# Gated outputs stored whole and split where they are read back, and weight factors made 512 columns at a time, in a gated pooling and recurrence block

## The chip, the cores and the metric

The kernel runs on one core of a Trainium2 chip. The metric is the device time of one execution in microseconds (us). The engines that matter here are TensorE (PE, which multiplies matrices and loads their weights), VectorE (DVE) and ScalarE (ACT), which work element by element, and SyncE (SP), on which this kernel issues nearly all its transfers. They run side by side, each in the order of its own list of instructions, and wait for each other through semaphores.

## The reference

One layer over 2048 tokens of 1024 channels: a norm, one wide projection h @ w_in, a pooling branch (branch A), a gated linear recurrence with 8 heads of 128 channels (branch B), a merge of both by sigmoid gates, an output projection and a residual. All is float32.

```python
def reference(x, c, w_ada, b_ada, g_pre, g_post, w_in, pool_w, pool_scale, lb_logits,
              hgrn_norm_g, w_pool_o, w_hgrn_o, w_out):
    ...
        h = rms_norm(x, g_pre[l]) * (1.0 + scale) + shift
        (pv, pg, hq, hf, hi, hg, mg_pool, mg_hgrn) = jnp.split(h @ w_in[l], split_idx, axis=-1)

        pooled = multiscale_pool(pv)
        pooled = jnp.einsum('bsgc,gcd->bsgd', pooled, pool_w[l].astype(jnp.float32))
        pooled = pooled.reshape(b, s, POOL_WIDTH) * pool_scale[l]
        branch_a = (pooled.astype(x.dtype) * jax.nn.silu(pg)) @ w_pool_o[l]
        ...
        f = lb + (1.0 - lb) * jax.nn.sigmoid(zf)
        ...
        o = hgrn2(q, k, v, logf)
        o = rms_norm(o, hgrn_norm_g[l]).astype(x.dtype).reshape(b, s, HGRN_WIDTH)
        branch_b = (o * jax.nn.silu(hg)) @ w_hgrn_o[l]

        merged = jax.nn.sigmoid(mg_pool) * branch_a + jax.nn.sigmoid(mg_hgrn) * branch_b
        y = merged @ w_out[l]
        x = x + gate * rms_norm(y, g_post[l])
```

The outputs that are gated, and that this change is about, are `pooled * silu(pg)` (called P in the kernel, 4 groups of 128 channels) and `o * silu(hg)` (called G, 8 heads of 128 channels).

## The kernel before

**Products.** Every large product is made from numbers split in two: `hi` is the value rounded to TensorE's fp32r form, `lo` what is missing. `split` makes the first on ACT with a copy and the second on DVE with a subtraction:

```python
    def split(src32, hi, lo, e=None):
        return A.copy(hi, src32), (e or V).tensor_tensor(lo, src32, hi.bitcast(F32), op=SUB)
```

`three` then multiplies hi by hi, hi by lo and lo by hi, so that one 128 by 512 by 128 product costs three matmuls. On top of it, blocks of two by two are multiplied with seven products in place of eight (a scheme of Strassen's kind). That is `quad` for the columns of w_in, and `rows7` for the projections to V and y of pass 1. The seven weight factors of such a block are sums and differences of its four quarters, named "11", "21", "12", "22" and "s1".

**Stages.** There are two passes (`p`) of 1024 tokens, each of two halves (`t`) of T = 512. In each pass V is made first. Then come the eight heads: for each head three quads, `fq` (gate f and q), `m` (the two merge gates, whose sigmoids go to DRAM as `Sd`) and `gp` (gate of the head, and pooling value or pooling gate). The last head has `gp` ahead of `m`. Between the products of a quad, `htick` runs a step of the recurrences of the head (`hgrn`, a generator for each half), so that the recurrence of head h runs inside the quads of head h and of the head behind. At its end it makes G (tile `sgg`, line 813). After the heads stand the **a jobs** (`a_job`, j = 0 to 7: P times w_pool_o, two halves of twelve matmuls each into the banks psA, then `sm` = psA times the sigmoid), the **b jobs** (the same with G and w_hgrn_o), and the projection to y.

**Gated outputs.** `two_out` splits an output. The last head's G and the last group's P stay on the chip. The others (heads 0 to 6, groups 0 to 2) are stored to the DRAM tiles Gd and Pd as hi and lo, two stores for each half. `two_in` reads them back: P in steps of the last head's `m` quad (`tick_in` takes one at each of the ticks, after two empty ones), G of head j - 1 ahead of the a job j.

**Weights.** `take` hands out the next weight and prepares four ahead (LOOK). In pass 0 a weight is loaded raw into `wr` (a pool of seven), combined on DVE where it is a factor, split into `whl` (a pool of four), and stored to DRAM as `scr_...`. Pass 1 reads these back, hi and lo in one load of 512 KB. For the projections to V and y in pass 1, the factors "v7" and "y7" are made beforehand by `row_factors`, whose 56 small steps hang behind the heads: "v7" in pass 0 and "y7" in pass 1. `htick` takes one at two of every five ticks:

```python
            if every[0] % 5 in (1, 3):
                once(behind_heads)
```

One group of seven steps is a load of two tiles (`ra`, `rb`), an empty step, and five steps of a sum and one or two splits (`put`). It works on 256 columns, hi and lo side by side in one tile `rf`. There are eight groups.

**What sets the order.** Each engine runs its instructions in program order as a scheduler laid them out, which puts an instruction where it expects its inputs to be ready. SP issues all transfers in one order. A transfer that waits for its data or for a free buffer holds those behind it. `gated` loads are placed behind the last store. All small tiles come from one pool of 76 (`utile`), the banks of the quads and of psA from a pool of four. In the profile L175 is the subtraction of `split` (or its copy on ACT), L109 a store, L179 a raw weight load, L461 (`tt`) any product, sum or difference of two tiles, L331 a matmul, L251 the sum that makes "s1" of a weight quad, and L684 and L690 the masked copies of the recurrence's scores.

## Time and profile before

| | us |
|---|---|
| median of three runs | 1799.85 |
| the three runs | 1799.85, 1803.84, 1798.95 |
| profiled execution, its own time | 1797.54 |
| span of its profile | 1795.8 |
| mean granted TensorE clock | 0.999 |
| heads of pass 0 | about 100 to 690 |
| a jobs of pass 0 | about 690 to 752 |
| heads of pass 1 | about 1016 to 1566 |
| a jobs of pass 1 | about 1566 to 1626 |

The profile is of one execution. Its page gives the busy time of each engine over the span. The trace behind it answers what one stretch of time, one tile or one wait holds. A row of a wait names the instruction that waited, its line, and what it waited for ("PE pagp L331 <- DVE c22gp L461"), then the total in us, the count and the longest. A row of the timeline gives the start in us, the time from start to end (neighbours may overlap), the engine (SPq is the queue of SP), the line, the operation, output and inputs, and the shape; a wait ahead of it stands in brackets.

### The profile page before, as it was taken

To read this page: it belongs to the slowest core of one execution; us is meant where nothing else is said; L and a number is where in the kernel's file an instruction comes from. 1 tells how busy PE (TensorE), PEld (TensorE's weight loads), DVE (VectorE), ACT (ScalarE), POOL (GpSimd) and SP (SyncE) were. 2 spreads that over 40 slices of the span, in tenths; PEclk is the share of its full clock that TensorE was granted. 3 is DMA by queue.
4 is the path that set the end of the run, shared out by engine and by line. 5 is a ranking of instruction groups with operands and counts; after the bars stand their busy time and mean duration, and the time that the engine had idled before them with its cause. 6 is when DMAs were issued, how large, how long until landed. Compare 5 with 4: busy or idle time off the path is not lost.

```text
span 1795.8 us, 32263 instructions
## 1 busy us (share of the span) xinstructions
PE 1753.0 (98%) x11997; PEld 1434.1 (80%) x11997; DVE 1161.1 (65%) x2522; ACT 801.1 (45%) x1925; POOL 80.6 (4%) x144
## 2 busy tenths in 40 slices
PE   7999999999999999999999999999999999999998
PEld 4787887888787787888878788888888888888886
DVE  3758898897888895475536166666666665633446
ACT  5746657566565563222433144354454453310041
POOL 1100000000000010000000000000000000000002
PEclk9999999999999999999999999999999999999999
DMA  9768787888878769997987886876877866696367
GB/s 316 255 198 292 272 295 288 277 304 281 285 271 300 265 213 318 336 323 257 320 294 249 281 254 199 282 249 215 274 228 238 280 206 238 201 351 209 129 204 258
DMA packets 270902, 471.49 MB, mean 263 GB/s; under 512 B 21101, under 2 KB 144666, under 8 KB 270746
## 3 DMA queue, kind: packets, MB, share of 16 engines
q1 hardware_dynamic: 270746, 469.44, 77.1%
q8 instruction: 94, 1.54, 0.4%
q14 instruction: 62, 0.51, 0.1%
HBM read 275.90 MB, written 193.46 MB: 261 GB/s over the span
## 4 chain that ended last, share of the span: by engine, by line
PE 62%; DMA 5%; DVE 2%; ACT 1%; issue 1%; SPq 0%; POOL 0%; DVEq 0%; ACTq 0%
PE psB L331 10%; PE pagp L331 6%; PE pam L331 6%; PE pafq L331 5%; PE psA L331 4%; PE psy L331 4%; PE pegp L331 3%; PE pefq L331 3%; PE pem L331 3%; PE psa L331 2%; PE ray L331 2%; PE po L331 2%; PE raV L331 2%; PE pbm L331 2%; PE pbfq L331 1%; PE pbgp L331 1%
## 5 line engine op out<-in xcount | busy, mean ns | idle before, releaser
L175 ACT CAST whl<-wr 128x512 fp32r<-128x512 f32 x192 | 118.5, 621 | 131.0 <-PE psB L331 24.7
L175 DVE TENSOR_TENSOR whl<-wr,whl 128x512 fp32r<-128x512 f32 x192 | 130.9, 688 | 64.2 <-ACT whl L175 55.2
L331 PE MATMUL psB<-Gh,whl 128*128 128x512 f32 x512 | 158.6, 390 | 0.0
L331 PE MATMUL pagp<-hT,whl 128*128 128x512 f32 x384 | 128.5, 395 | 4.7 <-DVE c22gp L461 3.8
L331 PE MATMUL pam<-hT,whl 128*128 128x512 f32 x384 | 129.5, 398 | 1.2 <-DVE c22m L461 1.2
L331 PE MATMUL pafq<-hT,whl 128*128 128x512 f32 x384 | 126.7, 391 | 3.3 <-ACT c12fq L592 3.3
L331 PEld LDWEIGHTS psB<-Gh,whl 128*128 128x128 f32 x512 | 96.1, 188 | 20.5 <-issue 0.5
L690 DVE COPY_PREDICATED PT<-mask,psa 128x256 f32<-128x256 uint8 x160 | 86.4, 550 | 36.1 <-PE psa L331 36.0
L331 PE MATMUL psB<-Gl,whl 128*128 128x512 f32 x256 | 100.0, 391 | 0.0
L331 PEld LDWEIGHTS pagp<-hT,whl 128*128 128x128 f32 x384 | 72.0, 188 | 21.9 <-issue 3.1
L331 PEld LDWEIGHTS pafq<-hT,whl 128*128 128x128 f32 x384 | 72.1, 188 | 19.5 <-ACT c12fq L592 4.4
L331 PEld LDWEIGHTS pam<-hT,whl 128*128 128x128 f32 x384 | 72.1, 188 | 17.2 <-DVE c22m L461 1.6
L331 PE MATMUL psA<-Ph,whl 128*128 128x512 f32 x256 | 82.5, 397 | 3.1 <-DMA Ph<-Pd 1.9
L331 PE MATMUL psV<-whl,hB 128*128 128x512 f32 x256 | 79.9, 394 | 2.4 <-ACT hB L175 2.4
L461 DVE TENSOR_TENSOR K<-K,TT 128x256 f32<-128x256 f32 x192 | 81.0, 426 | 1.8 <-PE psa L331 1.7
L331 PE MATMUL psy<-whl,mgh 128*128 128x512 f32 x256 | 80.4, 394 | 0.5 <-DVE y L461 0.5
L331 PE MATMUL pam<-lT,whl 128*128 128x512 f32 x192 | 74.9, 390 | 0.0
L331 PE MATMUL pagp<-lT,whl 128*128 128x512 f32 x192 | 74.9, 390 | 0.0
L331 PE MATMUL pafq<-lT,whl 128*128 128x512 f32 x192 | 74.7, 389 | 0.0
L331 PEld LDWEIGHTS psa<-X,K 128*32 128x32 f32 x2816 | 49.6, 110 | 25.8 <-issue 24.4
L461 DVE TENSOR_TENSOR sm<-psB,sm 128x512 f32<-128x512 f32 x32 | 22.0, 689 | 64.4 <-PE psB L331 63.9
L331 PE MATMUL psa<-X,K 128*32 128x48 f32 (+2 forms) x2816 | 60.3, 208 | 0.2 <-DVE PT L684 0.2
(471 smaller groups left out, 4417.2 us busy)
## 6 DMA issues: line engine op xcount, KB each, us to landing
wr<-in_w_in_dram SPq DMA_DIRECT2D x112, 256.0 KB, 5.0
whl<-scr_y SPq DMA_DIRECT2D x40, 512.0 KB, 4.9
sm<-Sd SPq DMA_DIRECT2D x64, 256.0 KB, 4.8
scr_v<-rfv SPq DMA_DIRECT2D x56, 256.0 KB, 2.8
whl<-scr_v SPq DMA_DIRECT2D x28, 512.0 KB, 3.7
scr_y<-rfy SPq DMA_DIRECT2D x56, 256.0 KB, 3.3
x<-in_x_dram SPq DMA_DIRECT2D x32, 256.0 KB, 4.9
wa<-in_w_ada_dram SPq DMA_DIRECT2D x32, 256.0 KB, 6.0
```

Source lines behind the costliest of these rows:

```text
L175: return A.copy(hi, src32), (e or V).tensor_tensor(lo, src32, hi.bitcast(F32), op=SUB)
L331: return PE.matmul(o, lhsT=l, rhs=r, start=start, stop=stop, skip_group_check=True)
L461: return (e or V).tensor_tensor(o, a, b, op=op)
L690: V.copy_predicated(dst.rearrange("p (c q) a b -> p c q a b", c=NT), m, src.rearrange("p c (a b) -> p c a b", b=b).unsqueeze(2) .broadcast ...
```

## The change

It has two parts. **Gated outputs**: `two_out` stores the output as it is (one store of 256 KB for each half in place of two, and the DRAM tiles are half as large). `two_in` reads it into the tile that will be `lo`, and the new `two_split` makes hi from it on ACT and then lo in place on DVE. For P the three splits are steps of the last head's `m` quad behind the loads (one empty step fewer, and what is left over is run after the quad); for G the split of head j - 2 is called ahead of the a job j, and that of head 6 after the last a job. What stays on the chip is split as before. **Weight factors**: `row_factors` works on 512 columns, in four groups of fourteen steps, with four loads of 256 KB, one operation of 512 columns in place of two of 256, and hi and lo in two tiles with a store each. The number of steps stays 56.

```diff
@@ -256,47 +256,41 @@
     def row_factors(key, src, e):
 
         steps = []
-        W = T // 2
         for i in range(4):
-            for c0 in (0, W):
-                r = {}
-
-                def put(f, nm, i=i, c0=c0, r=r):
-                    w = utile(f"rf{key}{f}{i}{c0}", F32R)
-                    hi, lo = w[:, 0:W], w[:, W:T]
-                    split(r[nm], hi, lo, e)
-                    if (key, f, i) not in scr:
-                        scr[key, f, i] = dram(f"scr_{key}_{f}_{i}", [P, 2 * T])
-                    store((key, f, i), scr[key, f, i].rearrange("p (z n) -> p z n", z=2)[:, :, c0:c0 + W],
-                          w.bitcast(F32).rearrange("p (z n) -> p z n", z=2))
-
-                def ld(i=i, c0=c0, r=r):
-                    a, b = utile(f"ra{key}{i}{c0}"), utile(f"rb{key}{i}{c0}")
-                    for w, k in ((a, 2 * i), (b, 2 * i + 1)):
-                        SP.dma_start(w.rearrange("p (z n) -> p z n", z=2),
-                                     src[k * P:(k + 1) * P, :].rearrange("p (z n) -> p z n", z=2)[:, :, c0:c0 + W])
-                    r.update({"11": a[:, 0:W], "21": a[:, W:T], "12": b[:, 0:W], "22": b[:, W:T]})
-
...
-                steps += [ld, nop, lambda two=two: two((0, "11"), (1, "12")),
-                          lambda two=two, a=sums: two(a, (2, "s1")),
-                          lambda two=two, a=sums2: two(a, (3, "11")),
-                          lambda two=two, a=sums3: two((4, "21"), a),
-                          lambda two=two: two((5, "12"), (6, "22"))]
+            r = {}
+
+            def ld(i=i, r=r):
+                for nm, k, z in (("11", 0, 0), ("21", 0, 1), ("12", 1, 0), ("22", 1, 1)):
+                    r[nm] = utile(f"ra{key}{i}{nm}")
+                    SP.dma_start(r[nm], src[(2 * i + k) * P:(2 * i + k + 1) * P, z * T:(z + 1) * T])
+
+            def put(f, nm, i=i, r=r):
+                w = [utile(f"rf{key}{f}{i}{z}", F32R) for z in range(2)]
+                split(r[nm], w[0], w[1], e)
+                scr[key, f, i] = dram(f"scr_{key}_{f}_{i}", [P, 2 * T])
+                for z in range(2):
+                    store((key, f, i), scr[key, f, i][:, z * T:(z + 1) * T], w[z].bitcast(F32))
+
+            def sums(r=r, i=i):
+                r["s1"] = utile(f"rs{key}{i}")
+                tt(r["s1"], r["21"], r["22"], op=ADD, e=e)
+
+            def sub(o, a, b, r=r):
+                tt(r[o], r[a], r[b], op=SUB, e=e)
+
+            nop = lambda: None
+            steps += [ld, nop, nop,
+                      lambda put=put: put(0, "11"),
+                      sums,
+                      lambda put=put: put(1, "12"),
+                      lambda put=put: put(2, "s1"),
+                      lambda sub=sub: sub("21", "11", "21"),
+                      lambda sub=sub: sub("11", "s1", "11"),
+                      lambda put=put: put(3, "11"),
+                      lambda put=put: put(4, "21"),
+                      lambda sub=sub: sub("12", "12", "11"),
+                      lambda put=put: put(5, "12"),
+                      lambda put=put: put(6, "22")]
         return steps
 
     early = {}
@@ -952,19 +946,24 @@
 
     def two_out(nm, p, i, t, src, cx, stay):
 
-        hi, lo = utile(f"{nm}h{p}_{i}_{t}", F32R), utile(f"{nm}l{p}_{i}_{t}", F32R)
-        split(src, hi, lo)
         if stay:
+            hi, lo = utile(f"{nm}h{p}_{i}_{t}", F32R), utile(f"{nm}l{p}_{i}_{t}", F32R)
+            split(src, hi, lo)
             cx["g" + nm][i, t] = (hi, lo)
         else:
-            for z, w in enumerate((hi, lo)):
-                store((nm, i), cx[nm + "d"][i][:, t, z, :], w.bitcast(F32))
+            store((nm, i), cx[nm + "d"][i][:, t, :], src)
 
     def two_in(nm, p, i, cx):
         for t in range(2):
-            cx["g" + nm][i, t] = tuple(utile(f"{nm}{z}{p}_{i}_{t}", F32R) for z in "hl")
-            for z, w in enumerate(cx["g" + nm][i, t]):
-                gated(w.bitcast(F32), cx[nm + "d"][i][:, t, z, :], (nm, i))
+            hi, lo = utile(f"{nm}h{p}_{i}_{t}", F32R), utile(f"{nm}l{p}_{i}_{t}", F32R)
+            raw = lo.bitcast(F32)
+            gated(raw, cx[nm + "d"][i][:, t, :], (nm, i))
+            cx["g" + nm][i, t] = (hi, lo)
+
+    def two_split(nm, i, cx):
+        for t in range(2):
+            hi, lo = cx["g" + nm][i, t]
+            split(lo.bitcast(F32), hi, lo)
 
     def sig_in(p, j, w, cx):
 
@@ -1155,9 +1154,9 @@
                               "mv", "y", "yss")}
         cx["Vd"] = dram(f"Vd{p}", [P, 8, D])
         for h in range(NH):
-            cx["Gd"][h] = dram(f"Gd{p}_{h}", [P, 2, 2, T])
+            cx["Gd"][h] = dram(f"Gd{p}_{h}", [P, 2, T])
         for g in range(NG):
-            cx["Pd"][g] = dram(f"Pd{p}_{g}", [P, 2, 2, T])
+            cx["Pd"][g] = dram(f"Pd{p}_{g}", [P, 2, T])
         for j in range(KT):
             for w in range(2):
                 cx["Sd"][j, w] = dram(f"Sd{p}_{j}_{w}", [P, 2, T])
@@ -1378,10 +1377,13 @@
                     quad("gp" + n, cx, gp, htick)
                 else:
                     if h == NH - 1:
-                        steps += [lambda: None] * 2
+                        steps += [lambda: None]
                         steps += [lambda g=g: two_in("P", p, g, cx) for g in range(NG - 1)]
+                        steps += [lambda g=g: two_split("P", g, cx) for g in range(NG - 1)]
                     quad("m" + n, cx, lambda row, t, u: m_got(p, h, row, t, u, cx), tick_in)
                 htick()
+            while steps:
+                once(steps)
             if p + 1 < NPASS:
                 x_stats(8 + h)
         while behind_heads:
@@ -1390,7 +1392,10 @@
         for j in range(KT):
             if j > 0:
                 two_in("G", p, j - 1, cx)
+            if j > 1:
+                two_split("G", j - 2, cx)
             a_job(p, j, cx)
+        two_split("G", NH - 2, cx)
         while active:
             tick()
         sums = []
```

The lines above 300 of the changed kernel stand six lines earlier: the masked copies at 684 and 690 are at 678 and 684, `tt` is at 455, the line of G at 807.

The scheduler lays the whole program out anew. Three places are shown. The first is DVE in head 4 of pass 0, in the `gp` quad, where G of head 3 is finished (sgg0_3). `whl133` and `whl134` are weight factors of this quad, `wrpv2_1` is one of its raw tiles, Gh and Gl are hi and lo of G, and rfv is a factor for V. Before:

```order
L813 SCALAR_TENSOR_TENSOR sgg0_3_0_4649<-pot0_3_0_5281,vec_102,sgg0_3_0_4649 128x512
L813 SCALAR_TENSOR_TENSOR sgg0_3_1_4591<-pot0_3_1_5293,vec_102,sgg0_3_1_4591 128x512
L175 TENSOR_TENSOR whl133_5312<-wrpv2_1_4960,whl133_5312 128x512
L175 TENSOR_TENSOR Gl0_3_0_5288<-sgg0_3_0_4649,Gh0_3_0_5287 128x512
L251 TENSOR_TENSOR wrpv2_1_4960<-wrpv2_1_4960,wrpv2_0_4953 128x512
L175 TENSOR_TENSOR Gl0_3_1_5300<-sgg0_3_1_4591,Gh0_3_1_5299 128x512
L175 TENSOR_TENSOR rfv732256_5306<-rav72256_4887,rfv732256_5306 128x256
L175 TENSOR_TENSOR whl134_5332<-wr13021_5196,whl134_5332 128x512
L690 COPY_PREDICATED PT0_141<-mask_98,psa0_0_1334 128x128x2
```

After:

```order
L807 SCALAR_TENSOR_TENSOR sgg0_3_0_4550<-pot0_3_0_5177,vec_102,sgg0_3_0_4550 128x512
L807 SCALAR_TENSOR_TENSOR sgg0_3_1_4501<-pot0_3_1_5184,vec_102,sgg0_3_1_4501 128x512
L175 TENSOR_TENSOR whl133_5194<-wrpv2_1_4856,whl133_5194 128x512
L251 TENSOR_TENSOR wrpv2_1_4856<-wrpv2_1_4856,wrpv2_0_4849 128x512
L175 TENSOR_TENSOR whl134_5214<-wr13021_5092,whl134_5214 128x512
L684 COPY_PREDICATED PT0_141<-mask_98,psa0_0_1334 128x128x2
```

The two Gl splits and the piece of a V factor are gone from in front of the split of whl134. The same place on SP, where wr13722 and wr13712 are raw weights of the head's next quad, before:

```order
L109 DMA Sd0_4_1_172<-sgm0_4_1_5278 128x512
L109 DMA Gd0_3_154<-Gh0_3_0_5287 128x512
L109 DMA Gd0_3_154<-Gl0_3_0_5288 128x512
L109 DMA Gd0_3_154<-Gh0_3_1_5299 128x512
L109 DMA Gd0_3_154<-Gl0_3_1_5300 128x512
L109 DMA scr_v7_3_2_4598<-rfv732256_5306 256x1x256
L109 DMA scr_('gp', 4)_3_5315<-whl133_5312 128x1024
L109 DMA scr_('gp', 4)_4_5335<-whl134_5332 128x1024
L179 DMA wr13722_5464<-in_w_in_dram 128x4x128
L179 DMA wr13712_5466<-in_w_in_dram 128x4x128
```

After:

```order
L109 DMA Sd0_4_1_172<-sgm0_4_1_5174 128x512
L109 DMA Gd0_3_154<-sgg0_3_0_4550 128x512
L109 DMA Gd0_3_154<-sgg0_3_1_4501 128x512
L109 DMA scr_('gp', 4)_3_5197<-whl133_5194 128x1024
L109 DMA scr_('gp', 4)_4_5217<-whl134_5214 128x1024
L179 DMA wr13722_5348<-in_w_in_dram 128x4x128
L179 DMA wr13712_5350<-in_w_in_dram 128x4x128
```

Ahead of the two raw loads there stand two stores of G in place of four, and no store of a V factor. The second place is SP in head 6 of pass 0, in the `fq` quad. Its factors are stored as scr_('fq', 6), and wr165 names the four raw tiles of the `m` quad behind it. Before:

```order
L109 DMA scr_('fq', 6)_3_6497<-whl161_6494 128x1024
L109 DMA scr_('fq', 6)_4_6517<-whl162_6514 128x1024
L109 DMA scr_('fq', 6)_5_6536<-whl163_6533 128x1024
L109 DMA scr_v7_0_3_5830<-rfv703256_6552 256x1x256
L109 DMA scr_v7_1_3_5835<-rfv713256_6556 256x1x256
L109 DMA scr_('fq', 6)_6_6563<-whl164_6560 128x1024
L179 DMA wr16511_6579<-in_w_in_dram 128x4x128
L179 DMA wr16521_6581<-in_w_in_dram 128x4x128
L179 DMA wr16522_6583<-in_w_in_dram 128x4x128
L179 DMA wr16512_6585<-in_w_in_dram 128x4x128
```

After:

```order
L179 DMA wr16511_6426<-in_w_in_dram 128x4x128
L179 DMA wr16521_6428<-in_w_in_dram 128x4x128
L109 DMA scr_('fq', 6)_3_6345<-whl161_6342 128x1024
L109 DMA scr_('fq', 6)_4_6365<-whl162_6362 128x1024
L109 DMA scr_('fq', 6)_5_6384<-whl163_6381 128x1024
L179 DMA wr16522_6430<-in_w_in_dram 128x4x128
L109 DMA scr_v7_3_3_6404<-rfv7330_6400 128x512
L109 DMA scr_v7_3_3_6404<-rfv7331_6401 128x512
L109 DMA scr_('fq', 6)_6_6410<-whl164_6407 128x1024
L179 DMA wr16512_6432<-in_w_in_dram 128x4x128
```

Two of the four raw loads moved ahead of the stores of factors 3 to 5, a third ahead of the stores of the V factor and of factor 6; the fourth stays behind them. The third place is DVE at the start of the a jobs of pass 0, where the recurrence of head 7 fills PT from its scores and scales K. Before:

```order
L690 COPY_PREDICATED PT0_141<-mask_98,psa0_0_1334 128x32x8
L461 TENSOR_TENSOR K0_7_0_7582<-K0_7_0_7582,TT0_7_0_7653 128x32x8
L684 COPY_PREDICATED PT0_141<-mask_98,psa0_0_1334 128x16x16
L461 TENSOR_TENSOR K0_7_0_7582<-K0_7_0_7582,TT0_7_0_7653 128x16x16
L684 COPY_PREDICATED PT0_141<-mask_98,psa0_0_1334 128x16x16
L690 COPY_PREDICATED PT1_142<-mask_98,psa0_1_1335 128x32x8
L461 TENSOR_TENSOR K0_7_1_7589<-K0_7_1_7589,TT0_7_1_7661 128x32x8
L684 COPY_PREDICATED PT1_142<-mask_98,psa0_1_1335 128x16x16
L461 TENSOR_TENSOR K0_7_1_7589<-K0_7_1_7589,TT0_7_1_7661 128x16x16
L684 COPY_PREDICATED PT1_142<-mask_98,psa0_1_1335 128x16x16
L175 TENSOR_TENSOR whl203_8209<-wr203_8207,whl203_8209 128x512
```

After:

```order
L684 COPY_PREDICATED PT0_141<-mask_98,psa0_0_1334 128x32x8
L455 TENSOR_TENSOR K0_7_0_7416<-K0_7_0_7416,TT0_7_0_7487 128x32x8
L175 TENSOR_TENSOR Pl0_0_0_7861<-Pl0_0_0_7861,Ph0_0_0_7860 128x512
L175 TENSOR_TENSOR Pl0_0_1_7864<-Pl0_0_1_7864,Ph0_0_1_7863 128x512
L678 COPY_PREDICATED PT0_141<-mask_98,psa0_0_1334 128x16x16
L455 TENSOR_TENSOR K0_7_0_7416<-K0_7_0_7416,TT0_7_0_7487 128x16x16
L678 COPY_PREDICATED PT0_141<-mask_98,psa0_0_1334 128x16x16
L684 COPY_PREDICATED PT1_142<-mask_98,psa0_1_1335 128x32x8
L455 TENSOR_TENSOR K0_7_1_7423<-K0_7_1_7423,TT0_7_1_7495 128x32x8
L678 COPY_PREDICATED PT1_142<-mask_98,psa0_1_1335 128x16x16
L455 TENSOR_TENSOR K0_7_1_7423<-K0_7_1_7423,TT0_7_1_7495 128x16x16
L678 COPY_PREDICATED PT1_142<-mask_98,psa0_1_1335 128x16x16
L175 TENSOR_TENSOR Pl0_1_0_7887<-Pl0_1_0_7887,Ph0_1_0_7886 128x512
L175 TENSOR_TENSOR Pl0_1_1_7890<-Pl0_1_1_7890,Ph0_1_1_7889 128x512
```

The splits of P of groups 0 and 1 (Pl0_0, Pl0_1, halves 0 and 1) now stand among these operations, the first pair behind two of them and the second behind eight more. In pass 1 one more order matters: before, the split of a factor for y (rfy753256) stood on DVE ahead of c22m of head 6, and in the changed order the factor's split there (rfy7631) stands behind it.

12 lines of the change are left out of this document (removed).

## The prediction

> **What bounds the kernel now.** I read the page first, then busy time by stage, then who waited for whom, then the timeline around the longest waits. The page:
>
> ```profile
> span 1795.8 us, 32263 instructions
> PE 1753.0 (98%) x11997; PEld 1434.1 (80%) x11997; DVE 1161.1 (65%) x2522; ACT 801.1 (45%) x1925; POOL 80.6 (4%) x144
> ```
>
> TensorE (PE) is busy for 1753.0 of 1795.8 us, and the change takes no matmul away. All that can be gained or lost is idle time of PE, 42.8 us in the whole run. The stages that the change touches are the heads (100 to 690 us in pass 0, 1016 to 1566 in pass 1) and the a jobs behind them:
>
> ```profile
> 100.00:690.00 590.00, 579.47 (x4539) 476.84 (x4538) 502.27 (x1127) 358.47 (x869) 30.28 (x42) 1.00 0.80 275
> 690.00:752.00 62.00, 58.93 (x402) 47.94 (x401) 25.75 (x51) 16.73 (x50) 3.27 (x6) 1.00 0.99 346
> 1016.00:1566.00 550.00, 547.40 (x4376) 451.91 (x4376) 335.26 (x831) 246.36 (x643) 17.61 (x28) 1.00 0.73 240
> 1566.00:1626.00 60.00, 58.78 (x404) 48.11 (x403) 22.01 (x45) 10.72 (x38) 2.40 (x4) 1.00 0.96 348
> ```
>
> Behind each stretch stand its length and the busy time of PE, weight load, VectorE (DVE), ScalarE (ACT) and POOL, then the granted clock (1.00 throughout), the share of the DMA engines and GB/s. In the heads of pass 0 DVE is busy 502 of 590 us and nearly bounds them too; in the a jobs the DMA engines are full (0.99 and 0.96). PE's idle time there is 10.5, 3.1, 2.6 and 1.2 us. The waits of PE, in the same order of stages (us in total, times, longest):
>
> ```profile
> PE pagp L331 <- DVE c22gp L461: 3.8, 3, 1.9
> PE pafq L331 <- ACT c12fq L592: 3.3, 4, 1.4
> PE pvm L331 <- ACT KS L777: 2.3, 2, 1.5
> ...
> PE psA L331 <- DVE sm L461: 1.2, 2, 0.9
> PE pk L775 <- DVE K L461: 1.1, 2, 0.7
> PE psA L331 <- DMA Ph<-Pd: 0.8, 1, 0.8
> ...
> PE pbfq L331 <- DMA whl<-scr_('fq', 0)_3_1356: 1.4, 1, 1.4
> PE pam L331 <- DVE c22m L461: 1.2, 1, 1.2
> ...
> PE psA L331 <- DMA Ph<-Pd: 1.1, 1, 1.1
> PE psA L331 <- DMA Pl<-Pd: 0.2, 1, 0.2
> ```
>
> They sum to 9.4, 3.1, 2.6 and 1.3 us: 16.4 us is the pool.
>
> **The change part by part.** *Factors 512 columns at a time.* Fewer, longer pieces on DVE:
>
> ```profile
> 599.34 0.75 DVE L175 TENSOR_TENSOR rfv<-rbv,rfv 128x256 fp32r<-128x256 f32 x2
> 600.01 0.42 DVE L461 TENSOR_TENSOR sq<-X,TT 128x256 f32<-128x256 f32 x1
> ...
> 458.94 0.69 DVE L175 TENSOR_TENSOR Gl<-sgg,Gh 128x512 fp32r<-128x512 f32 x1
> 459.54 0.68 DVE L251 TENSOR_TENSOR wrpv<-wrpv,wrpv 128x512 f32<-128x512 f32 x1
> 460.14 0.69 DVE L175 TENSOR_TENSOR Gl<-sgg,Gh 128x512 fp32r<-128x512 f32 x1
> ```
>
> Durations overlap, so I count from start to start: two of 256 columns take 600.01 - 599.34 = 0.67, or 0.335 each; one of 512 takes 0.60. Each pass has 56 half splits and 32 half sums, now 28 and 16 whole ones: 88 x 0.335 = 29.5 becomes 44 x 0.60 = 26.4, 3.1 us less. DMA counts and bytes stay.
>
> *Gated outputs unsplit.* Each pass moves 20 splits (7 heads and 3 groups, two halves) out of the heads: 20 x 0.60 = 12 us of DVE. With the factors DVE falls from 502 to about 487 us in pass 0. SyncE (SP) issues 20 stores of 256 KB fewer there and 20 loads fewer in the a jobs: 5.2 of the 62 x 346 = 21.5 MB that moved in pass 0's, about a quarter. The 20 splits go to the a jobs, where DVE was busy 25.75 of 62 us and is to be 37.8.
>
> Busy time of DVE is not PE's, so the gain must come wait by wait. The longest wait of the heads, in head 4 of pass 0, starts with a weight load that is issued late:
>
> ```profile
> 461.08 0.69 DVE L175 TENSOR_TENSOR whl<-wr,whl 128x512 fp32r<-128x512 f32 x1
> 462.55 1.05 SPq L109 DMA_DIRECT2D scr_('gp', 4)_4_5335<-whl  x1
> 463.65 1.82 SPq L179 DMA_DIRECT2D wr<-in_w_in_dram  x2
> 468.76 0.69 DVE L241 TENSOR_TENSOR wr137s<-wr,wr 128x512 f32<-128x512 f32 x1 [2.01 <-DMA wr<-in_w_in_dram]
> 473.14 0.68 DVE L461 TENSOR_TENSOR c22gp<-pagp,c22gp 128x512 f32<-128x512 f32 x1
> 473.98 0.47 PE L331 MATMUL pagp<-hT,whl 128*128 128x512 f32 x1 [1.90 <-DVE c22gp L461]
> ...
> 614.92 0.69 DVE L241 TENSOR_TENSOR wr179s<-wr,wr 128x512 f32<-128x512 f32 x1 [2.48 <-DMA wr<-in_w_in_dram]
> ```
>
> Both Gl splits stand ahead of the split of whl134 (461.08), whose store stands ahead of the load on SP. The load lands late, DVE idles 2.01 us at wr137s, c22gp is queued behind it, and PE waits 1.90 us. In the changed order the two Gl splits (1.2 us) and two of the four Gd stores are gone ahead of that point, so the load leaves at least 1.2 us earlier. I take 1.5 of the 1.9 us; in head 6, the same place (wr179s, 2.48 us), 1.2 us.
>
> In head 6 the four loads of wr165 leave at 563.14, behind four stores and their splits:
>
> ```profile
> 561.62 1.46 SPq L109 DMA_DIRECT2D scr_('fq', 6)_6_6563<-whl  x1
> 563.14 2.69 SPq L179 DMA_DIRECT2D wr<-in_w_in_dram  x4
> 568.72 0.69 DVE L175 TENSOR_TENSOR whl<-wr,whl 128x512 fp32r<-128x512 f32 x1 [1.39 <-DMA wr<-in_w_in_dram]
> 573.13 1.05 PE L331 MATMUL pvm<-pwt,pvt 128*128 128x128 f32 x7 [1.53 <-ACT KS L777]
> ```
>
> Two of them now stand ahead of all four stores and a third ahead of the last. The whole 1.5 us should go. The third c22gp wait (3.8 - 1.9 - 1.5, from the other two) is DVE's load alone: 0.3. Heads of pass 0: -1.5 - 1.2 - 1.5 - 0.3 = **-4.5 us**.
>
> Pass 1's c22m wait is a factor split that waits for ScalarE in front of it:
>
> ```profile
> 1473.85 0.42 DVE L175 TENSOR_TENSOR rfy<-rby,rfy 128x256 fp32r<-128x256 f32 x1 [2.37 <-ACT rfy L175]
> 1474.20 0.68 DVE L461 TENSOR_TENSOR c22m<-pam,c22m 128x512 f32<-128x512 f32 x1
> ```
>
> In the changed order this factor's split stands behind c22m: **-1.2 us**.
>
> *The a jobs.* Three groups must now be split before the matmuls, a new wait on PE's path. The Pl0 subtractions stand on DVE behind a mask copy and a K product, those of group 1 behind eight more such operations.
>
> ```profile
> 693.62 0.43 DVE L690 COPY_PREDICATED PT<-mask,psa 128x256 f32<-128x256 uint8 x1 [1.83 <-PE psa L331]
> 693.83 0.50 PE L331 MATMUL psA<-Ph,whl 128*128 128x512 f32 x1
> 711.63 16.65 PE psA L331 x72
> ```
>
> The last row, of the chain of waits, gives 16.65 / 72 = 0.231 us a matmul. First split: 693.62 + 2 x 0.335 + 0.69 = 694.98, while PE has three matmuls from 693.83 and is done at 694.52, so 0.5 us of waiting. Group 1: two splits from 694.29, eight operations and 0.69: 694.29 + 1.20 + 2.68 + 0.69 = 698.86, against 694.98 + 12 x 0.231 = 697.75 and about half a microsecond of scores: 0.6. So +1.1 us, if P lands by 694; its loads are half as many and the same store now stands behind the first pair. Of the old 3.1 us the Ph and K waits (1.9) go, since the scores' operands are ready by then, and the sm wait stays. Pass 0: 1.1 - 1.9 = **-0.8**. In pass 1 DVE has no weights to split and group 0 is split before its scores, so group 1 costs about 0.3 instead of 1.3: **-1.0**. The 14 G splits cost nothing so long as they fit beside DVE's idle 24 us; with that cover gone they cost as in the slower rival.
>
> *What is late next.* Some 2500 DVE rows change their order. Below, the 5 us of pass 0 that I left alone (9.4 - 4.5) could shrink as well; above, each of ten waits on DVE or ACT in the heads could grow by a longer piece, 10 x 0.265 = 2.7. I take one new wait as long as the three that go (1.9, 1.5, 1.5): **+1.6**.
>
> Sum: -4.5 - 1.2 - 0.8 - 1.0 + 1.6 = -5.9 us on the profiled execution's 1797.54 us (span 1795.8 and 1.7 around it): 1791.6. The median of the three runs shown is 1799.85, 2.3 above that, so I forecast 1793.9. A measurement of this kernel tells 0.3%, 5.4 us, from no change; the forecast stands just beyond that line (1794.45).
>
> **The rivals.**
> *Waits move on.* SP runs in order: a load placed earlier can still block there until its buffer of the seven raw ones is free, and c12fq (3.3 us) stands next in line. Against it: the removed stores and splits are real work. Then only the a jobs' 1.8 is kept, less the new 1.6: about 1799.6.
>
> *Everything goes.* The 16.4 us of the four stages vanish: 1783.5. For it: DVE is relieved by 15 us in pass 0. Against it: the c12fq waits and a weight load that is late in pass 1 (1.4) are not touched.
>
> *Longer pieces.* A piece of 512 columns holds DVE 0.265 us longer than a half, and PE has ten such waits: 2.7 us back, 1796.6. The longest waits above start with a late load, not with a piece, which speaks against it. The Trainium skill (Perfetto Trace Analysis, Optimizing Scalar/DVE Operations) says that where these engines are not saturated but cause bubbles on others, breaking up instructions may let work finish sooner; the change does the reverse, and by that rule this rival would hold. The trace shows no bubble that a half piece caused, so it has a small chance.
>
> *Slower: G splits hold the evictions.* On DVE the G splits stand between the sm products that free psA's banks.
>
> ```profile
> Gh<-Gd SPq DMA_DIRECT2D x14, 256.0 KB, 6.9
> DVE sm L461 <- DMA sm<-Sd: 17.5, 5, 5.1
> ```
>
> A G load takes 6.9 us to land there, one a job takes 24 x 0.231 = 5.5. If SP issues it only a job ahead, DVE stands still 1.4 us at each of 14 places, and if the two spare banks give no cover, PE does too: 19.6 - 5.9 + 1.8 = 15.5 us more, 1815. It decides once landing passes two jobs, 11 us, for then the spare banks are used up. Against it: a quarter of the bytes is gone, and DVE already waits 17.5 us for sm while PE loses only 1.2.
>
> That the change doesn't do what it says is excluded: the changed order has the 80 DMAs fewer and the splits where the code puts them.
>
> **How the numbers follow.** Forecast 0.50, its own range 1789 to 1797.5 (the two bounds of the new waits, and the a jobs' gain gone); everything goes 0.12; waits move on 0.21; longer pieces 0.08; slower 0.09. From 1787 to 1803 the forecast, the moving waits and the longer pieces lie inside, about 0.8. Faster by over 0.3%: 0.6 of the forecast's 0.50, and 0.12: 0.42. Within: the rest of the forecast, 0.21 and 0.08: 0.49. Slower: 0.09.
>
> **What would show it.** In the profile after: no wait of a microsecond before pagp in heads 4 and 6, none at pvm in head 6 and none on c22m in head 6 of pass 1; wr137s and wr179s without two microseconds of DMA wait; DVE near 487 us in the heads of pass 0; a wait of PE on a Pl split, half a microsecond each, at the start of the a jobs of pass 0; DMA share of the a jobs below 0.9. Wrong would be new waits of several microseconds in the heads at loads whose buffer is not free, or DVE standing at Gl splits while psA waits for a bank.

## The result, and the profile after

| | before | after |
|---|---|---|
| median | 1801.6 us of 4 runs (1798.95 to 1803.84) | 1782.8 us of 4 runs (1781.45 to 1784.67) |
| ratio | | 0.9897, 95% interval 0.9878 to 0.9916 |
| profiled execution, own time | 1797.54 | 1784.67 |
| span of its profile | 1795.8 | 1782.9 |

The change makes the kernel 18.8 us faster by the medians. A second comparison gave 13.6 us and a ratio of 0.9923 (0.9907 to 0.9940), and the two pairs of profiled executions that are compared below lie 12.9 and 14.9 us apart. So the size is known to some 5 us. The forecast was 1793.9 and its range ended at 1787. The rival in which all waits of the four stages vanish gave 1783.5.

The page of the changed kernel shows nearly the same work of PE, and 88 instructions of DVE fewer:

```profile
span 1782.9 us, 31954 instructions
PE 1751.9 (98%) x11997; PEld 1436.1 (81%) x11997; DVE 1153.7 (65%) x2434; ACT 795.4 (45%) x1869; POOL 81.3 (5%) x144
```

Busy time of the heads and of the a jobs of pass 0, in the same columns as in the prediction:

```profile
100.00:690.00 590.00, 586.70 (x4630) 483.25 (x4629) 490.10 (x1070) 349.46 (x830) 30.62 (x42) 1.00 0.78 271
690.00:752.00 62.00, 62.00 (x362) 51.90 (x361) 39.51 (x73) 25.72 (x67) 3.69 (x6) 1.00 0.98 318
```

DVE fell by 12 us in the heads of pass 0 and rose by 14 in the a jobs, where PE now has no idle time at all. The share of the DMA engines in the heads is hardly lower, 0.78 against 0.80. Two of PE's waits in the heads of pass 0 before the change stand behind the dots in the prediction's list:

```profile
PE pagp L331 <- DVE pm L461: 0.8, 1, 0.8
PE psa L331 <- DVE PT L684: 0.2, 1, 0.2
```

With them the heads held 10.4 us of waits, not 9.4, and the pool of the four stages was 17.4 us. PE's waits in the heads of pass 0 after the change, first of this profile, then of a second one of the same kernel:

```profile
PE pagp L325 <- DVE c22gp L455: 1.1, 2, 0.6
PE pvm L325 <- ACT KS L771: 0.8, 2, 0.5
PE pafq L325 <- ACT c12fq L586: 0.6, 1, 0.6
PE psA L325 <- ACT Ph L175: 0.5, 1, 0.5
```

```profile
PE pagp L325 <- DVE c22gp L455: 1.1, 2, 0.6
PE psA L325 <- ACT Ph L175: 0.5, 1, 0.5
```

Of 10.4 us of waits 3.0 and 1.6 are left. One row of PE's waits in pass 1 is new, at the start of its a jobs:

```profile
PE psA L325 <- DMA whl<-scr_a: 1.2, 1, 1.2
```

**Where the time went, stage by stage.** All kernels here have the same 11997 matmuls, so the start of the n-th can be compared between two traces. Each number below is how much the lag against the first profile of before grew over a stage (the median lag of 60 matmuls at each end). All rows are of one profile each. The column "start" is the first 50 us.

| kernel | start | heads, pass 0 | a jobs, pass 0 | up to head 0 of pass 1 | heads 1 to 7, pass 1 | a jobs, pass 1 |
|---|---|---|---|---|---|---|
| before, second profile | +0.2 | -0.9 | -0.6 | -0.5 | -0.1 | -0.3 |
| after | +2.5 | -8.2 | -3.7 | -1.1 | -1.4 | -0.6 |
| after, second profile | +0.3 | -9.3 | -3.7 | -2.2 | -1.4 | -0.7 |
| forecast | 0 | -2.9 | -0.8 | 0 | -1.2 | -1.0 |

The forecast's heads of pass 0 are -4.5 and the new wait of +1.6. The start is the same code in both kernels; its 0.2 to 3.4 us in the eighteen profiles that are compared with the first are chance, and so is about a microsecond of each other column. The miss is in two places: 5.3 to 6.4 us in the heads of pass 0, 2.9 us in the a jobs of pass 0.

### The profile page after: what moved, and what is told of

Read it like the earlier page. It is cut to its first block, busy times and chain, and to the rows that moved or that the text cites. A ratio compares the mean times of both kernels' runs of the same rounds, so it can differ in the third digit from the quotient of the medians.

```text
span 1782.9 us, 31954 instructions
## 1 busy us (share of the span) xinstructions
PE 1751.9 (98%) x11997; PEld 1436.1 (81%) x11997; DVE 1153.7 (65%) x2434; ACT 795.4 (45%) x1869; POOL 81.3 (5%) x144
## 4 chain that ended last, share of the span: by engine, by line
PE 85%; DVE 5%; DMA 5%; ACT 2%; issue 2%; SPq 1%; POOL 0%; DVEq 0%; ACTq 0%; POOLq 0%
PE psB L325 10%; PE pam L325 9%; PE pafq L325 8%; PE pagp L325 8%; PE psA L325 5%; PE psV L325 5%; PE pem L325 4%; PE psy L325 4%; PE pefq L325 4%; PE pegp L325 4%; PE psa L325 3%; PE po L325 3%; PE ray L325 2%; PE pbfq L325 2%; PE pbm L325 2%; PE pbgp L325 2%
## 5 line engine op out<-in xcount | busy, mean ns | idle before, releaser
L325 PEld LDWEIGHTS psV<-whl,hB 128*128 128x128 f32 x256 | 48.2, 191 | 16.3 <-ACT hB L175 4.9
```

Of the source, the lines that this page charges most:

```text
L325: return PE.matmul(o, lhsT=l, rhs=r, start=start, stop=stop, skip_group_check=True)
```

## Experiments

The change is in two parts, so each part was run alone, then pieces of each. The table gives what was measured, the texts behind it what was expected. The ratio is to the kernel before on the same chip, whose median lay between 1797.1 and 1801.6. The last columns are lags as above. With each edit the scheduler lays the program out anew, so a lag of a microsecond is not read.

| kernel | median, us | ratio, interval | heads, pass 0 | a jobs, pass 0 |
|---|---|---|---|---|
| before_again | 1795.01, one run | | -0.9 | -0.6 |
| changed_again | 1783.58 | 0.9923 (0.9907 to 0.9940) | -9.3 | -3.7 |
| unsplit_only | 1788.86 | 0.9954 (0.9939 to 0.9969) | -3.9 | -3.7 |
| unsplit_again | 1789.38, one run | | -3.8 | -3.7 |
| factors_only | 1795.09 | 0.9989 (0.9980 to 0.9998) | -2.5 | -0.8 |
| stored_twice | 1796.74 | 0.9979 (0.9968 to 0.9990) | -2.3 | -1.7 |
| split_in_heads | 1782.52 | 0.9899 (0.9885 to 0.9914) | -11.0 | -3.1 |
| heads_whole | 1796.09 | 0.9980 (0.9969 to 0.9991) | -2.6 | -1.7 |
| pool_whole | 1792.51 | 0.9957 (0.9942 to 0.9972) | -1.6 | -2.9 |
| two_stores | 1786.16 | 0.9925 (0.9902 to 0.9948) | -7.3 | -3.7 |
| wide_store | 1789.72 | 0.9944 (0.9922 to 0.9967) | -3.3 | -3.7 |
| half_pieces | 1784.97 | 0.9918 (0.9896 to 0.9940) | -8.4 | -3.6 |
| rows_early | 1800.69 | 0.9999 (0.9985 to 1.0012) | +1.1 | -1.9 |
| whole_2k | 1794.88 | 0.9967 (0.9954 to 0.9980) | -4.6 | -3.7 |
| before_2k | 1805.37 | 1.0027 (1.0012 to 1.0041) | +1.5 | -0.5 |
| factors_stored_whole | 1786.19 | 0.9924 (0.9906 to 0.9941) | -10.4 | -3.7 |
| old_form_new_steps | 1789.90 | 0.9941 (0.9918 to 0.9964) | -6.4 | -3.7 |

**The two parts.** Edit: only the hunks of `two_out`, `two_in`, `two_split` and the DRAM tiles, or only that of `row_factors`.

> Only the gated outputs are stored whole; the weight factors are made 256 columns at a time as before. Theory 1 (the splits and transfers that leave the heads carry the gain): 13 to 16 us less than before, about 1786; heads of pass 0 by 6 us shorter or more, a jobs of pass 0 by 3 shorter, the 1.2 us wait of pam in head 6 of pass 1 still there. Theory 2 (the factors' longer pieces and fewer rows on DVE and SP carry about half): only 6 to 9 us less, with the a jobs' 3 us among them, and waits of 1 us and more at pagp of heads 4 and 6 still there.

> Only the weight factors are made 512 columns at a time; the gated outputs are split before they are stored, as before. Theory 1: 1 to 3 us less than before, of which 1.2 to 1.5 is the pam wait in head 6 of pass 1; heads of pass 0 within 2 us of before. Theory 2: 6 to 9 us less, nearly all in the heads of pass 0; the a jobs of pass 0 as before.

The gated outputs' part carries more than half (8.3 of the 13.6 us on the same chip), and the whole gain in the a jobs. The factors' part is worth 0.1% alone (0.02 to 0.2%). In the heads of pass 0 the parts give 3.9 and 2.5 us alone and 8.2 to 9.3 together, 2 to 3 us more than their sum. Neither theory holds as it was put. One reason for the surplus is seen at pvm of head 6: with the factors alone this wait is 2.9 us, against 1.5 and 0.8 in the two profiles of before; with both parts it is at most 0.5.

**Second profiles.** No edit.

> The changed kernel once more, for a second profile. If the 2.5 us by which the first profile began its products later than the profile of before are chance, they are within 1 us here; if they belong to the change, they come again. Time 1781 to 1785.

> The kernel before once more, for a second profile. If the waits of the heads are fixed by the order of the instructions, the heads of pass 0 come out within 1 us of the first profile and the waits of 1.9, 1.5 and 1.5 us stand at the same places; if they hang on how transfers happen to land, they move by a microsecond or more.

The start's 2.5 us were chance (0.3 here). Before came out 0.9 us shorter in the heads of pass 0, with the c22gp waits at the same places and sizes (1.9 and 1.5 us in heads 4 and 6). The waits of c12fq and pvm moved between the two profiles by up to 1.1 us each, which would fit transfers behind them but doesn't show it.

**Transfers or VectorE?** The edits on the changed kernel:

```diff
-            store((nm, i), cx[nm + "d"][i][:, t, :], src)
+            for z in range(2):
+                store((nm, i), cx[nm + "d"][i][:, t, z, :], src)
```

for stored_twice, with two loads in `two_in`, and for split_in_heads, in the same branch:

```diff
+            eh, el = utile(f"e{nm}h{p}_{i}_{t}", F32R), utile(f"e{nm}l{p}_{i}_{t}", F32R)
+            split(src, eh, el)
             store((nm, i), cx[nm + "d"][i][:, t, :], src)
```

> The changed kernel, but each gated output that goes to DRAM is stored twice and read back twice (into both tiles), so that the number and the bytes of the transfers are those of before; the splits stay where the change puts them. Theory A (the transfers ahead of a late load on SP set the waits of the heads): 6 us or more of the gain is lost, about 1790, with waits of 1 us and more back at pagp of head 4 or at c12fq in the heads of pass 0, and 2 to 3 us back in the a jobs of pass 0. Theory B (DVE's splits in the heads set them): within 3 us of the changed kernel in the heads, and only the a jobs lose 1 to 3.

> The changed kernel, but each gated output is also split where it is made, into two tiles that nobody reads; transfers are those of the changed kernel. Theory A: within 3 us of the changed kernel. Theory B: 5 us or more of the gain is lost in the heads of pass 0, with DVE busy some 500 us there again and waits of 1 us and more at pagp of heads 4 and 6.

Busy time by stage of the heads of pass 0, first stored_twice, then split_in_heads (DVE is the third figure behind the comma):

```profile
100.00:690.00 590.00, 581.99 (x4548) 479.31 (x4547) 487.22 (x1064) 345.21 (x823) 30.86 (x42) 1.00 0.80 276
```

```profile
100.00:690.00 590.00, 588.11 (x4641) 484.99 (x4640) 502.87 (x1098) 362.84 (x853) 31.88 (x42) 1.00 0.78 272
```

With DVE no busier than in the changed kernel (487 us against 490), the transfers of before take back 6 to 7 us of the heads. With DVE as busy as before (503 us), nothing is lost. Theory A stands: DVE's splits cost PE nothing in the heads. The total of stored_twice came out above the 1790 expected, since the later stages lost too.

**Which wait hangs on which store?** Only G or only P stored whole.

> Of the change only G is stored whole; P is split before it is stored, and the factors are as before. If each output acts on the waits behind its own stores: the c22gp waits of heads 4 and 6 fall from 3.4 us to about 1.5, as with both outputs whole, the c12fq wait of head 4 (1.1 to 1.25 us, behind P's stores of head 3) stays, and the a jobs of pass 0 keep the 0.8 us wait for Ph. If it is only the sum of the load: both kinds of wait fall by some two thirds. About 4 to 6 us less than before.

> Of the change only P is stored whole; G is split before it is stored, and the factors are as before. If each output acts on the waits behind its own stores: the c12fq wait of head 4 goes, the c22gp waits of heads 4 and 6 stay above 1 us each, and the a jobs lose their waits for Ph and K but keep the one for sm. If it is only the sum of the load: each kind of wait falls by a third. About 2 to 4 us less than before.

The c22gp wait of head 4, behind G's stores of head 3, is 0.52 us with G whole and 1.89 with P whole; that of head 6 is 0.92 and 1.57. So G acts on the waits behind its own stores. The c12fq wait of head 4 (1.25 us before) is 0.57 us with G whole and gone with P whole. But with P whole ACT's order differs there too, so that P's stores are the cause is not shown (see the c12fq waits below). In the a jobs P does most: with P whole no sm wait is left, against what was expected, and the only wait is a new one of 0.5 for ACT's copy to Ph. By the medians the two give 3.8 and 7.4 us, against 4 to 6 and 2 to 4 expected. That is more than the 8.3 of both, but each of these figures is uncertain by 2 us or more, so that an overlap of the two is not shown.

**Bytes or number of stores?** The edits on the changed kernel, two_stores and wide_store:

```diff
-            store((nm, i), cx[nm + "d"][i][:, t, :], src)
+            for z in (0, 64):
+                store((nm, i), cx[nm + "d"][i][z:z + 64, t, :], src[z:z + 64, :])
```

```diff
-            store((nm, i), cx[nm + "d"][i][:, t, :], src)
+            store((nm, i), cx[nm + "d"][i][:, t, :, :], src.unsqueeze(1).broadcast_to([P, 2, T]))
```

> The changed kernel, but each gated output that goes to DRAM leaves in two stores of 64 partitions each (128 KB), so that SP issues as many stores as before while the bytes stay those of the change; loads are those of the change. If the number of stores on SP sets the waits of the heads: about 1789, with 4 us or more of the gain in the heads of pass 0 lost. If the bytes do: within 2 us of the changed kernel.

> The changed kernel, but each gated output that goes to DRAM is written twice by one store of 512 KB, so that the bytes written are those of before while the stores on SP are as few as with the change; only one copy is read back. If the bytes set the waits of the heads: about 1789, with 4 us or more of the gain in the heads of pass 0 lost. If the number of stores does: within 2 us of the changed kernel.

The bytes count for more: twice the bytes take back 5 to 6 us of the heads, twice the stores 1 to 2. The place in head 4 shows how. SP's queue and DVE in the changed kernel:

```profile
453.35 0.41 SPq L109 DMA_DIRECT2D scr_('gp', 4)_2_5160<-whl  x1
453.86 0.40 SPq L109 DMA_DIRECT2D Sd<-sgm  x1
454.35 1.87 SPq L109 DMA_DIRECT2D Gd<-sgg  x2
456.32 0.58 SPq L109 DMA_DIRECT2D scr_('gp', 4)_3_5197<-whl  x1
456.99 0.58 SPq L109 DMA_DIRECT2D scr_('gp', 4)_4_5217<-whl  x1
457.63 2.52 SPq L179 DMA_DIRECT2D wr<-in_w_in_dram  x2
...
464.32 0.69 DVE L241 TENSOR_TENSOR wr137s<-wr,wr 128x512 f32<-128x512 f32 x1 [1.75 <-DMA wr<-in_w_in_dram]
```

and in wide_store, where the same rows stand in the same order:

```profile
455.52 0.40 SPq L109 DMA_DIRECT2D scr_('gp', 4)_2_5160<-whl  x1
456.01 0.41 SPq L109 DMA_DIRECT2D Sd<-sgm  x1
456.50 1.91 SPq L109 DMA_DIRECT2D Gd<-sgg  x2
458.51 1.18 SPq L109 DMA_DIRECT2D scr_('gp', 4)_3_5197<-whl  x1
459.78 1.15 SPq L109 DMA_DIRECT2D scr_('gp', 4)_4_5217<-whl  x1
460.98 2.98 SPq L179 DMA_DIRECT2D wr<-in_w_in_dram  x2
...
467.43 0.69 DVE L241 TENSOR_TENSOR wr137s<-wr,wr 128x512 f32<-128x512 f32 x1 [2.06 <-DMA wr<-in_w_in_dram]
```

The second figure of an SPq row is how long SP took to issue. The stores of G take 1.9 us in both, but the two factor stores behind them take 1.18 and 1.15 us in place of 0.58 each. So SP took longer to issue behind more bytes, and the load of wr137 went out later. The table gives, in us from the start of the store of factor 2, when the load of wr137 was issued and when wr137s began, and then PE's wait on c22gp:

| | load issued after | wr137s after | PE waits |
|---|---|---|---|
| before | 7.9 | 13.0 | 1.90 |
| P whole alone | 8.2 | 13.0 | 1.89 |
| stored_twice | 6.0 | 11.9 | 1.00 |
| wide_store | 5.5 | 11.9 | 0.98 |
| two_stores | 5.4 | 11.3 | 0.35 |
| G whole alone | 5.4 | 11.2 | 0.52 |
| after | 4.3 | 11.0 | 0.52 |
| split_in_heads | 4.6 | 10.9 | 0.46 |

The issue is only part of it. In two_stores and wide_store the load goes out at the same time (5.4 and 5.5), yet wr137s comes 0.6 us later behind twice the bytes, and PE waits 0.6 us longer. So the bytes ahead also lengthen the time from the load's issue to wr137s (5.9 and 6.5 us). The change brought the issue forward by 3.6 us, far more than the 1.2 of the prediction's working, but wr137s by only 2.0. PE's wait can be compared only where DVE has the same rows between wr137s and c22gp: it takes 4.9 us between them in after, G whole and split_in_heads and 4.4 in the other five, so the small waits of two_stores and after don't rank. The other waits that come back in wide_store (pvm of head 4, 1.5 us; one of pm, 1.6) were not followed back row by row.

**Longer pieces.** On the changed kernel each sum and split of a factor is done twice on 256 columns:

```diff
-                split(r[nm], w[0], w[1], e)
+                for c in (slice(0, T // 2), slice(T // 2, T)):
+                    split(r[nm][:, c], w[0][:, c], w[1][:, c], e)
```

> The changed kernel, but every sum and split of the weight factors is done in two pieces of 256 columns on DVE and ACT; tiles and transfers are those of the change. If longer pieces hold up DVE and ACT: 1 to 3 us less than the changed kernel. If the waits hang on the transfers: within 2 us of it, though DVE is 3 us and ACT some 5 us busier in the heads of pass 0.

The heads of pass 0 came out as with the change (-8.4). So neither the longer pieces nor the shorter busy time that they give DVE matters here. By the rule quoted in the prediction (the Trainium skill, Perfetto Trace Analysis, Optimizing Scalar/DVE Operations) short pieces might have helped; the run shows no gain here.

**The c12fq waits.** They were left alone in the forecast. In head 2 of before, SP, ACT and PE show this:

```profile
259.89 1.15 SPq L109 DMA_DIRECT2D scr_('fq', 2)_2_2862<-whl  x1
263.43 1.18 SPq L109 DMA_DIRECT2D scr_v<-rfv  x2
264.67 1.10 SPq L114 DMA_DIRECT2D x<-in_x_dram  x2
...
269.13 0.63 ACT L469 ACTIVATE jx<-x 128x512 bf16<-128x512 f32 x1 [1.52 <-DMA x<-in_x_dram]
...
270.68 0.56 ACT L592 COPY c12fq<-pafq 128x512 f32<-128x512 f32 x1
...
271.29 0.50 PE L331 MATMUL pafq<-hT,whl 128*128 128x512 f32 x1 [1.38 <-ACT c12fq L592]
```

ACT stands at the sum of squares of a row of x (jx, a statistic for pass 1) until its load lands, and the copy that PE needs is queued behind it. The load is late because the stores of V factors ahead of it on SP wait for their data: SP issued nothing from 261.04 to 263.43. In head 4 it is the same (a V factor's store at 408.09 after 2.3 us without an issue, the load of x at 408.70). In head 6 P's two stores stand there, and wait for their splits. The change did not act on all of these in the same way. In head 2 the V factor's stores now stand behind the load, which is issued at 259.12. In head 4 a V factor's store still stands ahead of it, and ACT still stands 1.16 us, at the second row of x (411.25); but the copy c12fq now comes between the two rows and starts at 409.50, while PE needs it at 411.98. So there it was the new order that saved the copy: behind both rows, as before, it would have come too late, since the second row's work ends only at 411.98. To test the load of x alone, on the kernel before:

```diff
             for i, kind in enumerate(KINDS[h == NH - 1]):
+                if i == 1 and p + 1 < NPASS:
+                    xrows = x_rows(8 + h, SP.dma_start)
...
-                x_stats(8 + h)
+                x_stats(8 + h, xrows)
```

> The kernel before, but the rows of x whose squares ACT sums for pass 1 in each head of pass 0 are loaded ahead of the last quad of that head and not behind it. If the c12fq waits of heads 2, 4 and 6 come from ACT standing at a late load of x: these three (2.0 to 2.8 us in the two profiles of before) fall to under 0.5 us, the c22gp waits of heads 4 and 6 stay above 1 us each, and the kernel is 1 to 3 us faster. If they come from DVE or from ACT's own load, they stay.

The three c12fq waits are gone, as expected. But the scheduler put jx ahead of another copy, c12gp, and PE waits for that one. The c22gp waits of heads 4 and 6, which were to stay, are replaced by it:

```profile
PE pagp L331 <- ACT c12gp L592: 6.9, 4, 2.1
```

```profile
249.99 0.63 ACT L469 ACTIVATE jx<-x 128x512 bf16<-128x512 f32 x1 [4.62 <-DMA x<-in_x_dram]
...
251.89 0.58 ACT L592 COPY c12gp<-pagp 128x512 f32<-128x512 f32 x1
```

That ACT stands at the load of x and passes the wait on to PE is shown; loading earlier is no remedy. ACT stood 4.62 us at the load, which here left behind four stores of G. The total is that of before, not 1 to 3 us less.

**Why the factors' part helps.** A store of a factor took SP 0.52 us before and 0.34 with rows of 2 KB (min, median and longest of 56, in ns; first before, then factors_only):

```profile
L109 SPq DMA_DIRECT2D scr_v<-rfv x56: 518/519/2269, 144.8 to 602.5; - x56
```

```profile
L109 SPq DMA_DIRECT2D scr_v<-rfv x56: 319/338/1131, 155.0 to 600.9; - x56
```

That is 56 x 0.18 = 10 us of SP, so it was tried alone, with hi and lo of a piece side by side in DRAM:

```diff
-                    store((key, f, i), scr[key, f, i].rearrange("p (z n) -> p z n", z=2)[:, :, c0:c0 + W],
-                          w.bitcast(F32).rearrange("p (z n) -> p z n", z=2))
+                    store((key, f, i), scr[key, f, i][:, 2 * c0:2 * c0 + T], w.bitcast(F32))
```

> The gated outputs stored whole, and the weight factors made 256 columns at a time as before, but each of their stores writes rows of 2 KB (hi and lo of a piece side by side in DRAM) in place of two rows of 1 KB; pass 1 reads them back in rows of 1 KB and in two loads each, which costs there what it costs. If the factors' part of the gain comes from SP, which issues a store of 2 KB rows in 0.34 us and one of 1 KB rows in 0.52 (medians of the two profiles), the heads of pass 0 come out 6.5 us or more shorter than before, against 3.9 with the outputs whole alone. If it comes from where the pieces of 512 columns stand, about 4.

> The kernel before with the same edit to the factors' stores alone. If SP's time to issue them is the cause, the heads of pass 0 come out 2 to 3 us shorter, as with the factors alone; if the order of the pieces is, within 1 us of before.

It isn't that. The edit did shorten SP's issue (medians 0.38 us in whole_2k and 0.35 in before_2k), but -4.6 us in the heads is near the -3.9 and -3.8 without it, and before_2k has even lost 1.5. The Trainium skill (Perfetto Trace Analysis, DMA Optimizations) says that small DMAs, under 2 KB, carry a significant overhead each. These stores move 256 KB each, and only their rows are of 1 KB. Read of rows, SP's issue time agrees with it, 0.52 against 0.34 us, but PE doesn't feel it in this stage. Next, the old form at the new place, four groups of fourteen steps with both halves in one step:

> The changed kernel, but the weight factors keep their old form (pieces of 256 columns, hi and lo in one tile, loads and stores in rows of 1 KB) while their steps stand where the change puts them: four groups of fourteen, one sum or one factor a step. If it is the place of the steps that shortens the heads of pass 0, these come out 8 to 10 us shorter than before, as with the change; if it is the form of the pieces and rows, some 4 to 5, as with the outputs whole alone.

> The kernel with the gated outputs stored whole alone, for a second profile: its heads of pass 0 came out 3.9 us shorter than before. If that is what this part does, 3 to 5 us here; if a chance profile, further off, and then the sum of the two parts has to be read anew.

The heads came out at -6.4, between -3.9 and -8.2, and neither expectation holds. It is one profile, and two of one kernel differ by about a microsecond, so this says only that the place of the steps gives some of what the factors' part adds beside the other. The rest goes with the form of tiles and transfers, and which feature of it isn't settled: the length of the pieces showed no effect, nor did the rows of the stores with the steps at their old place; the rows of the loads and the tiles weren't tried alone. In pass 1 the c22m wait of head 6 is back in half_pieces (1.19 us) and in half in old_form_new_steps (0.59). It hangs on which row the scheduler lays ahead of c22m: in half_pieces again a factor's split that waits 2.4 us for ACT, and in factors_stored_whole below, in head 1, a product of the recurrence that waits as long.

**Bytes once more.** On the changed kernel the factors too are stored unsplit and split where they are read back:

```diff
-                split(r[nm], w[0], w[1], e)
-                scr[key, f, i] = dram(f"scr_{key}_{f}_{i}", [P, 2 * T])
-                for z in range(2):
-                    store((key, f, i), scr[key, f, i][:, z * T:(z + 1) * T], w[z].bitcast(F32))
+                scr[key, f, i] = dram(f"scr_{key}_{f}_{i}", [P, T])
+                store((key, f, i), scr[key, f, i], r[nm])
```

> The changed kernel, and the weight factors too are stored unsplit (28 stores of 256 KB in place of 56 in each pass) and split where they are read back. If bytes ahead of late loads are what the heads of pass 0 lose time to, these come out 1 to 2 us shorter still; the 28 splits go to the projections to V and y of pass 1, where nobody has shown cover for them. Total between 3 us less and 3 us more than the changed kernel.

Its waits in the heads of pass 0:

```profile
PE psA L327 <- ACT Ph L175: 0.5, 1, 0.5
PE psa L327 <- DVE PT L680: 0.2, 1, 0.2
```

No c22gp, c12fq or pvm wait of a size that this view shows is left there, and the stage is 1 to 2 us shorter than with the change, as forecast, though that is hardly more than two profiles of one kernel differ by. The projection to V of pass 1 pays for it (+1.3 us from the b jobs of pass 0 to V, where the change has -0.7 and -2.5), so that the total is no better than the changed kernel's.

## Why the prediction was wrong

*What bounds the kernel: right. The pool: a microsecond too small.* The 9.4 us of the heads left out the pm and PT waits (0.8 and 0.2), so the pool was 17.4 us and not 16.4. The change took nearly all of the larger waits.

*Head 4 and head 6, late weight loads: right in size, and in mechanism but for DVE's share.* The c22gp wait of head 4 fell from 1.90 to 0.52 us (forecast 1.5 less), that of head 6 from 1.46 to 0.63 (forecast 1.2 less), the third went (forecast 0.3 less). The pvm wait of head 6 fell from 1.53 (0.84 in the second profile of before) to 0.46 and in the second profile vanished (forecast: gone). Together these gave 3.8 and 4.2 us of the 4.5. But the working gave the two Gl splits of DVE 1.2 us of the credit; split_in_heads shows that they cost nothing, and wide_store that the bytes count. DVE still stands at wr137s and wr179s for 1.75 and 1.85 us (2.01 and 2.48 before), so the sign under "What would show it", no two microseconds, came only by the letter: the loads are earlier, and DVE is there earlier too. What counts is that wr137s starts 2.0 us sooner behind the store of factor 2 (13.0 and 11.0 in the table).

*"The 5 us of pass 0 that I left alone": this step failed.* The rest of the pool in the heads, 5.9 us with the two missing rows, was not looked at row by row, and the sum took nothing for it. The c12fq waits (3.3 us in the first profile, 2.9 in the second), the pvm wait of head 2 (0.8 and 1.4) and the pm wait (0.8 and 0.2) went down to 0.6 and less. Less the new ones, these made the waits of the heads fall by another 3.9 and 4.6 us in the two profiles of the change, against the first of before. "The c12fq waits ... are not touched" is wrong: three of the four are ACT standing at a late load of x, and that load is in the same queue as the stores that the change moves and halves. How it went is in part luck: in head 2 the load came earlier, in head 4 it was ACT's new order that saved the copy. Why the pvm wait of head 2 and the pm wait fell was not followed back.

*"One new wait as long as the three that go", +1.6: did not come at that size.* The only waits at new places in the heads are c12fq in head 5 (0.57 and 0.14), pvm in head 4 (0.30, then none; the second profile of before has 0.24 there too), and two of 0.1 us.

*The a jobs of pass 0, -0.8 forecast, -3.7 measured: this step failed too.* The Ph and K waits (1.9) went as forecast. The new split wait was put at 1.1 and is one of 0.45, on ACT's copy. The Pl splits of group 1 stand behind eight other operations, as forecast, but came just in time for their matmul at 693.84. Ahead of it PE had sixteen matmuls of psA and 1.0 us of the recurrence's scores, where the working had fifteen and half a microsecond:

```profile
688.68 1.29 DVE L175 TENSOR_TENSOR Pl<-Pl,Ph 128x512 fp32r<-128x512 f32 x2
...
692.56 2.48 DVE L175 TENSOR_TENSOR Pl<-Pl,Ph 128x512 fp32r<-128x512 f32 x4
```

The sm wait (1.2), which was to stay, went too. 1.9 + 1.2 - 0.45 = 2.65 of the 3.7 are so accounted for; the rest is no single wait. The share of the DMA engines there was to fall below 0.9 and is 0.98, though they moved 318 GB/s in place of 346.

*Pass 1: about right.* The c22m wait went (forecast -1.2, stage -1.4), by the order as it was said; but that is luck of the order, since half_pieces, which only halves the pieces, has the wait back. In the a jobs Ph's wait was replaced by one for the weight scr_a (1.2 us), and the stage gave 0.6 to 0.7 of the 1.0.

*Slower by G's splits: did not come.* DVE stood at 39.5 us of 62 in the a jobs of pass 0, near the 37.8 of the forecast, and PE does not wait there.

*The chances.* "Everything goes" had 0.12, and the measured time is within a microsecond of it. That the number fits so well is in part luck: its four stages gave 13.9 and 15.1 us in the two profiles, not the 17.4 that they held, waits of 0.5 to 1.2 us are left or new, and the rest of the 18.8 lies outside these stages. The mechanism given for it, DVE relieved by 15 us, isn't the cause in the heads, as split_in_heads shows. What speaks for it stood in the trace: the weight loads and the loads of x with which the c22gp and c12fq waits begin are all in SP's queue, behind stores that the change halves or moves.

## What to carry to other kernels

When all transfers go through one queue, follow every wait of the bound engine back to the load behind it, and count the bytes that stand ahead of that load, and look whether a store ahead of it waits for its data. Here 512 KB of stores less ahead of a weight load (two stores of 256 KB) shortened PE's wait, and the VectorE time that went with them was worth nothing in that stage. Storing a value once at full width and splitting it where it is read back is then a gain, if the reading stage has idle time on VectorE and ScalarE. A load moved ahead in the same queue may only move the wait to the next instruction of the engine that reads it.

## What the runs showed of the hardware

The time that SP needs to issue a transfer isn't fixed. The same store of a factor (512 KB) took 0.58 us behind two stores of 256 KB (0.60 in the second profile) and 1.18 behind two of 512 KB; a store of a V factor ranges from 0.52 to 2.27 us in one profile. Nor does the mean share of the DMA engines tell it: 0.78 in the heads of the changed kernel and 0.80 before, with PE idle for 3 us in the one and 10 in the other.
